# Where the expert biases are prepared, which expert groups come first, and how the smallest groups use the PE columns in a decoder layer

## The chip, the core and the metric

The kernel runs on one core of a Trainium2 chip. Its engines are TensorE (PE, with its weight loads shown apart as PEld), VectorE (DVE), ScalarE (ACT), GpSimd (POOL) and SyncE (SP), which here issues all DMA transfers. The metric is the device time of one execution in microseconds; smaller is better. The profile's rows show the TensorE clock as a granted share of 2.4 GHz: 1.00, or 0.50, which is 1.2 GHz.

## The reference

One decoder layer on 256 tokens of width 1024: a mixer (8 heads of forgetting attention and 4 mLSTM heads, then one output product), cross-attention into 256 memory tokens, and a top-4-of-32 mixture of experts, each followed by a layer norm of `alpha*x + part`. Cut to what matters here:

```python
mixed = jnp.concatenate([fo, mo_out], axis=-1)          # (256, 1024)
x = layer_norm(ALPHA * x + mixed @ w_out, ln1_g, ln1_b)
x = layer_norm(ALPHA * x + cross_attention(x, mem), ln2_g, ln2_b)
logits = x @ w_router + b_router                        # (256, 32)
top_vals, top_idx = lax.top_k(logits, 4)
gates = softmax(top_vals)
for e in range(32):                                     # the tokens that chose e
    h = xe @ w_gate_up[e] + b_gate_up[e]                # 1024 -> 2048
    g, l = minimum(h[:, :1024], 7), clip(h[:, 1024:], -7, 7)
    y[tokens] += gate * ((g * sigmoid(1.702 * g) * (l + 1)) @ w_down[e] + b_down[e])
x = layer_norm(ALPHA * x + y, ln3_g, ln3_b)
```

All weights are float32. One expert has 12 MiB of them: 8 MiB gate/up and 4 MiB down.

## The kernel before

**Slots and the weight stream.** SBUF holds 24 slots of 1 MiB (`NU = 24`). `big()` takes the slot that has been free longest, `done()` puts slots back at the end of that list. All large tiles live there: weight chunks, their split halves, activations, the table of expert biases `bgf`. Weights come as a stream of 1 MiB chunks in a fixed order (`stream`): the projections, the two *static* experts 0 and 1 (16 gate/up chunks, then 8 down chunks), and then the other experts in an order found at run time, each one's 8 gate/up chunks ahead of the previous one's 4 down chunks. `pump()` takes a slot for the next chunk and issues its DMA on SP's queue (L143 to L149) as long as slots are free. SP works in order: a DMA into a slot whose last user isn't done holds up everything that SP issues after it. Which instruction comes when on each engine is fixed ahead of time by a scheduler that goes by program order; `tc.high_priority(offset=-300)` makes instructions rank as if they stood 300 places later, a positive offset as if they stood earlier.

**Front.** Projections, the head groups, the mixer's output product with the first layer norm (from L640 on, `take_sq`, `apply_N`, `stats`, `layer_norm`), cross-attention (`queries`, `xattn`), its output product (`attn_out`) and the router (`logits`, `router`). Float32 products of the front are made of three products of split halves: `split()` makes the high half on ACT (L173) and the low half on DVE (L176).

**Expert biases.** `b_gate_up` is added by a bf16 matmul with a selector column (L1196), so the float32 table is cut into three bf16 parts on partitions 0 to 63, 64 to 95 and 96 to 127 of `bgu`. Before the change the table is loaded after the second half of the cross-attention (L744), and POOL cuts it into parts during the attention's output product (L820 to L823). The first expert's bias matmuls read `bgu`.

**Experts.** The tokens of an expert are put into a group of 32, 64, 96 or 128 places (T, S, M, B). After the routing, experts are ranked by their count of tokens, and the 32 groups of the table `BATCHES` are given to them by size; each batch has 256 places (the first 128), and the order in the table is the order of work. The 32nd group is worked on only if its expert has tokens, so 31 run. `gate_up(i)` makes bias and gate/up product with the tokens as the stationary operand and the weights as the moving one, 512 columns at a time: for 64 places two column halves of PE work side by side (`128*64`), for 32 places four quarters (`128*32`), for 128 places the whole array. M runs as S and T. `turned(i)` transposes the hidden rows into `hT` (a half slot, always at its start), and `product(i-1)` multiplies by the down weights; T has only two column groups there, on partitions 0 to 31 and 32 to 63. ACT and DVE copy the two output halves into `y`. `fillers(i)` between experts makes the one-hot matrices, gathers the next batch's tokens (L918), scatters finished rows into the result (L1113), and after item 2 starts the accumulator (`start_acc`).

Of the kernel before, what the change touches and what calls it, by code (L numbers as in the profile page):

```python
# [12 lines left out]
BF = mybir.dt.bfloat16  # L13
I32 = mybir.dt.int32
AF = mybir.ActivationFunctionType
ALU = mybir.AluOpType
# [5 lines left out]
KT = 8  # L22
# [8 lines left out]
NSTATIC = 2  # L31
T, S, M, B = 32, 64, 96, 128

BATCHES = [[S] * NSTATIC, [S, S, M, T], [B, T, T, T, T], [S, S, M, T], [B, S, S], [M, T, S, S], [M, T, S, S],
           [M, T, T, T, T, T]]
NU = 24
NT2 = 8
# [12 lines left out]
def layer_kernel(ctx, tc, x, mem, w_in, fox_f_bias, conv_w, i_bias, f_bias, fox_g, mlstm_g, w_mix,  # L50
                 ln1_g, ln1_b, w_xq, w_xk, w_xv, w_xo, ln2_g, ln2_b, w_router, b_router,
                 w_gu, b_gu, w_dn, b_dn, ln3_g, ln3_b, out):
    nc = tc.nc
# [6 lines left out]
    cp = ctx.enter_context(tc.tile_pool(name="cp", bufs=1))  # L60
# [14 lines left out]
    def big(shape, dt=F32, last=False):  # L75

        i = free.pop(-1 if last else 0)
        t = up.tile(shape, dt, name=nm("u"), tag=f"u{i}")
        owner[id(t)] = (i, t)
        return t  # L80

    def done(*ts):
        for t in ts:
            free.append(owner.pop(id(t))[0])
# [12 lines left out]
    def t2(shape, dt=F32):  # L97
        return wk.tile(shape, dt, name=nm("t2"), tag="t2", bufs=NT2)
# [484 lines left out]
    done(vmo, fvm)  # L583


    def stats(t, n, st):

        ve.bn_stats(st[:, n], xs[:, t, 512 * n:512 * n + 512])
        if n == 0:
            return  # L590
        mv = sm([128, 2])
        ve.bn_aggr(mv, st)
        rs = sm([128, 2])
        se.activation(rs[:, 0:1], mv[:, 1:2], AF.Ln, bias=eps_l)
        se.activation(rs[:, 1:2], rs[:, 0:1], AF.Exp, scale=-0.5)
        return mv[:, 0:1], rs[:, 1:2]
# [7 lines left out]
    def take_sq(W=None, n=4, ahead=4, reserve=2):  # L604

        W = W or ([], [])
        for i in range(n):
            ch = take()
            pump(taken[0] + ahead, reserve)
            with tc.high_priority(offset=-300):  # L610
                W[0].append(split(ch, 4, 512))
            W[1].extend(W[0][-1])
        return W
# [25 lines left out]

    ln1 = load_ln(ln1_g, ln1_b)  # L640
    W, Wh = take_sq()
    pump(taken[0] + 4)
    sts = [sm([128, 2, 6]) for _ in range(2)]
    for n in range(2):
# [94 lines left out]
    heads(1)  # L739
    Wo[0, 1] = take_xo()  # L740
    done(qT)
    bgf = big([128, 2048])
    for q in range(4):
        nc.sync.dma_start(bgf[32 * q:32 * q + 32], b_gu)  # L744
    pump(len(stream), 2)


# [67 lines left out]
    ve.tensor_scalar(rsum, pb[:, 0], -1.0, None, op0=ALU.mult)  # L815
    ve.tensor_copy(brow_, pb[:, 1])
    ve.tensor_tensor(wr, wr, g2[:, :, None].to_broadcast([128, KT, NE]), op=ALU.mult)

    bgu = cp.tile([128, 2048], BF, name="bgu", tag="shared")
    gp.tensor_copy(bgu, bgf)  # L820
    for q in (64, 96):
        gp.tensor_tensor(bgf[q:], bgf[q:], bgu[q:], op=ALU.subtract)
        gp.tensor_copy(bgu[q:], bgf[q:])  # L823
    done(bgf)

    gp.memset(lgx, -3e38)
    gdpos = cp.tile([128, 2, 2, NE], F32, name="gdpos")
    pump(len(stream))
# [324 lines left out]
        given[0] += 1  # L1153
        pump(1 << 20, held_back[0] if given[0] > 4 else 0)

    def transposed(hid):

        out_, at = [], 0
        hT = half_slot(0)
        for hh in hid:  # L1160
            n = hh.shape[0]
            p = bank((4, 5), [128, 4, n])
            for j in range(4):
                te.transpose(p[:, j], hh[:, j * 128:(j + 1) * 128], ident[0:n, 0:n])  # L1164
            o = hT[:, at:at + 4 * n].rearrange("p (k s) -> p k s", s=n)
            se.copy(o, p)  # L1166
            out_.append(o)
            at += 4 * n
        return out_
# [49 lines left out]
        hidden[i] = hid  # L1219

    def turned(i):
        hidden[i] = transposed(hidden[i])

    def product(i):

        b, o = starts[i]
        c = flat[i]
        gk = (b, o // 128)
        hT = hidden.pop(i)
        if gk not in Y:  # L1230
            Y[gk] = half_slot(1)
            if i == nitem - 1:
                gp.memset(Y[gk], 0.0)
            elif gk == (len(BATCHES) - 1, 1):
                gp.memset(Y[gk][96:128], 0.0)  # L1235
        y = Y[gk]
        work = []
        for m, (a, n) in enumerate(parts(c)):
            if n == B:
                p = [bank((4, 5), [128, 512]) for _ in range(2)]  # L1240
                work.append((a, n, p, lambda k: hT[k // 4][:, k % 4]))
            else:
                p = bank((4, 5), [128, 512])
                work.append((a, n, [p[n * h:n * h + n] for h in range(2)],
                             lambda k, m=m, n=n: hT[m][:, k % 4, n * (k // 4):n * (k // 4) + n]))
        for k2 in range(KT // 2):
            cd = next_chunk()
            for a, n, p, w in work if k2 % 2 == 0 else work[::-1]:
                for kk in range(2):
                    k = 2 * k2 + kk  # L1250
                    for h in range(2):
                        te.matmul(p[h], w(k), cd[:, kk, 512 * h:512 * h + 512], start=(k == 0), stop=(k == KT - 1),  # L1252
                                  skip_group_check=True)
            give(cd)
        for a, n, p, _ in work:
            q = (o + a) % 128
            se.copy(y[q:q + n, 0:512], p[0])  # L1257
            ve.tensor_copy(y[q:q + n, 512:1024], p[1])  # L1258
        if (o + c) % 128 == 0 or i >= nitem - 2:
            pend.append(gk)  # L1260
# [212 lines left out]
```

## Time and profile before

| what | value |
|---|---|
| median of 3 runs | 1217.68 us (1217.25 to 1220.58) |
| profiled execution | 1217.34 us, span of its instructions 1215.5 us |
| mean granted TensorE clock | 0.975 |
| PE / DVE / ACT / POOL busy share of the span | 94% / 31% / 19% / 4% |
| HBM read | 428.18 MB |

The span runs from the first to the last instruction of the program; 1.84 us of the profiled execution lie around it. All places in time below are microseconds from the span's start. In a row of the timeline, the last bracket is the engine's idle time before the instruction and what ended it. A matmul that is written once in the program appears as two instructions when its operands are float32. Several matmuls overlap in the array, so the time of a run of them is read from the row's total, not from one instruction.

### The profile page before, as it was taken

The page shows a single profiled execution, that of the slowest core. Times are in us where ns is not written, and L with a number is a line of the kernel's source. Part 1 is how long each engine was busy: PE and PEld are TensorE (multiplying, and loading weights), DVE is VectorE, ACT ScalarE, POOL GpSimd, SP SyncE. Part 2 cuts the span into 40 slices and gives each one's busy share as a digit, 9 for nine tenths or more (in the row PEclk, how much of TensorE's full clock was granted, in tenths as well). Part 3 has the DMA queues.
Part 4 walks back from the last instruction along what each step waited for, and adds up shares of the span by engine and source line. Part 5 has one row for each costly group of instructions (what it writes and reads, how often), then busy time and mean ns, then how long its engine had stood idle before and what let it go on. Part 6 is the DMA issues. An engine that isn't in the chain of part 4 may idle for free.

```text
span 1215.5 us, 14844 instructions
## 1 busy us (share of the span) xinstructions
PE 1141.2 (94%) x5825; PEld 524.4 (43%) x5826; DVE 376.9 (31%) x775; ACT 230.9 (19%) x429; POOL 49.2 (4%) x79
## 2 busy tenths in 40 slices
PE   9999999979999999999899899999999999999875
PEld 8997678855443334332223333433233323322211
DVE  6674656462323120421120302222211222122212
ACT  5545534311200110111001100110111010100101
POOL 3320000040000000000000000000000000000000
PEclk9999999987998999999999999999999999999888
DMA  8763328576999999999999999999999999999994
GB/s 284 273 224 123 139 99 304 224 243 218 375 377 372 416 401 360 377 417 417 417 417 416 417 417 417 417 417 416 417 417 417 416 417 417 416 417 417 417 416 176
DMA packets 92104, 430.25 MB, mean 354 GB/s; under 512 B 11152, under 2 KB 11704, under 8 KB 60158
## 3 DMA queue, kind: packets, MB, share of 16 engines
q1 hardware_dynamic: 92030, 429.26, 88.7%
q8 instruction: 47, 0.77, 0.3%
q14 instruction: 27, 0.22, 0.0%
HBM read 428.18 MB, written 1.05 MB: 353 GB/s over the span
## 4 chain that ended last, share of the span: by engine, by line
PE 76%; DMA 17%; DVE 5%; ACT 1%; issue 1%; SPq 0%; DVEq 0%; ACTq 0%
PE ps L1202 28%; PE ps L1252 18%; PE ps L195 14%; DMA u<-in_w_gate_up_dram 10%; DMA u<-in_w_down_dram 7%; PE ps L1113 4%; PE ps L918 2%; PE ps L1164 1%; DVE t L1132 1%; PE ps L1196 1%; PE ps L694 1%; PE ps L715 1%; PE ps L513 1%; DMA u<-in_w_mix_out_dram 1%; PE ps L478 1%
## 5 line engine op out<-in xcount | busy, mean ns | idle before, releaser
L1202 PE MATMUL ps<-u,u 128*64 128x512 f32 (+2 forms) x2304 | 441.6, 604 | 13.4 <-DMA u<-in_w_gate_up_dram 13.2
L1252 PE MATMUL ps<-u,u 128*64 128x512 f32 (+2 forms) x1152 | 287.3, 601 | 5.3 <-DMA u<-in_w_down_dram 2.4
L1202 PEld LDWEIGHTS ps<-u,u 128*64 128x64 f32 (+2 forms) x2304 | 136.0, 127 | 283.6 <-issue 223.7
L195 PE MATMUL ps<-u,u 128*128 128x256 f32 (+1 forms) x1152 | 200.8, 327 | 0.5 <-DVE u L184 0.5
L195 PEld LDWEIGHTS ps<-u,u 128*128 128x128 f32 x1152 | 165.7, 191 | 20.3 <-issue 3.3
L1252 PEld LDWEIGHTS ps<-u,u 128*64 128x64 f32 (+2 forms) x1152 | 79.7, 127 | 169.4 <-issue 147.8
L1128 DVE TENSOR_SCALAR t<-ps 128x512 f32<-128x512 f32 (+1 forms) x38 | 26.1, 686 | 377.2 <-PE ps L1202 377.2
L1258 DVE COPY u<-ps 64x512 f32<-64x512 f32 (+2 forms) x36 | 24.8, 690 | 262.6 <-ACT u L1257 238.1
L1130 ACT ACTIVATE t<-t 128x512 f32<-128x512 f32 (+1 forms) x38 | 23.9, 630 | 343.8 <-DVE t L1128 343.8
L176 DVE TENSOR_TENSOR u<-u,u 128x1024 fp32r<-128x1024 f32 x58 | 74.2, 1310 | 19.8 <-ACT u L173 13.7
L173 ACT CAST u<-u 128x1024 fp32r<-128x1024 f32 x64 | 64.9, 1049 | 40.7 <-PE ps L195 16.2
L1257 ACT COPY u<-ps 64x512 f32<-64x512 f32 (+2 forms) x36 | 20.7, 576 | 249.9 <-PE ps L1252 233.7
L1113 PE MATMUL ps<-u,gt 128*128 128x512 f32 x112 | 59.3, 639 | 5.4 <-ACT u L1257 5.4
L1115 DVE TENSOR_TENSOR u<-u,ps 128x512 f32<-128x512 f32 x56 | 38.5, 687 | 57.6 <-PE ps L1113 57.6
L923 ACT ACTIVATE u<-ps,pcol 128x256 f32<-128x256 f32 (+1 forms) x60 | 29.9, 553 | 73.3 <-PE ps L918 63.7
L918 PE MATMUL ps<-t,u 128*128 128x256 f32 (+1 forms) x256 | 41.3, 307 | 0.2 <-ACT u L923 0.2
L1196 PE MATMUL ps<-bgu,selb 128*64 128x512 bf16 (+2 forms) x143 | 25.8, 397 | 16.2 <-DVE t L1132 15.5
L918 PEld LDWEIGHTS ps<-t,u 128*128 128x128 f32 x256 | 34.4, 199 | 15.1 <-issue 10.4
L1166 ACT COPY u<-ps 128x512 f32<-128x512 f32 (+1 forms) x38 | 18.6, 488 | 93.4 <-PE ps L1164 93.1
L1113 PEld LDWEIGHTS ps<-u,gt 128*128 128x128 f32 x112 | 18.5, 193 | 39.7 <-issue 14.9
L1235 POOL MEMSET u<- 32x1024 f32 x1 | 0.9, 947 | 844.6 <-PE ps L1113 844.6
L1164 PEld LDWEIGHTS ps<-ident,t 128*128 128x128 f32 (+1 forms) x152 | 14.4, 139 | 31.9 <-issue 16.8
(274 smaller groups left out, 609.6 us busy)
## 6 DMA issues: line engine op xcount, KB each, us to landing
u<-in_w_gate_up_dram SPq DMA_DIRECT2D x248, 1024.0 KB
u<-in_w_down_dram SPq DMA_DIRECT2D x122, 1024.0 KB
u<-in_w_in_dram SPq DMA_DIRECT2D x20, 512.0 KB
u<-in_w_xk_dram SPq DMA_DIRECT2D x4, 1024.0 KB
u<-in_w_xv_dram SPq DMA_DIRECT2D x4, 1024.0 KB
u<-in_w_mix_out_dram SPq DMA_DIRECT2D x4, 1024.0 KB
u<-in_w_xq_dram SPq DMA_DIRECT2D x4, 1024.0 KB
u<-in_w_xo_dram SPq DMA_DIRECT2D x4, 1024.0 KB
```

Source lines behind the costliest of these rows:

```text
L173: a = se.copy(h[:, sl], c[:, sl])
L176: b = eng.tensor_tensor(l[:, sl], c[:, sl], h[:, sl].bitcast(F32), op=ALU.subtract)
L195: m = te.matmul(out, wsl(wp[a]), xsl(xp[b]), start=(first and i == 0), stop=(last and i == 2), skip_group_check=True)
L918: te.matmul(p[:, j], s[:, t, k * 128:(k + 1) * 128], oh[b][:, t], start=(t == j == i == 0), stop=(t == 1 and s is src[-1]), skip_group_che ...
L923: a = se.activation(xg[b][:, k, 0:cols], p[:, j], AF.Identity, scale=g2[:, k:k + 1], bias=b2[:, k:k + 1])
L1113: te.matmul(p, gth[gk][:, t], y[:, 512 * n:512 * n + 512], start=True, stop=True)
L1115: ve.tensor_add(a, a, p)
L1128: ve.tensor_scalar(g, G, LIMIT, None, op0=ALU.min)
L1164: te.transpose(p[:, j], hh[:, j * 128:(j + 1) * 128], ident[0:n, 0:n])
L1196: te.matmul(out_[q], selb[:, r:r + 1].to_broadcast([128, n]), bgu[:, 512 * q:512 * q + 512], start=True, stop=False, skip_group_check=True)
L1202: te.matmul(out_[q], X[:, k, o + a:o + a + n], ch[:, 512 * q:512 * q + 512], start=False, stop=(k == KT - 1), skip_group_check=True)
L1252: te.matmul(p[h], w(k), cd[:, kk, 512 * h:512 * h + 512], start=(k == 0), stop=(k == KT - 1), skip_group_check=True)
```

## The change

Three edits, made together. The table `b_gate_up` is loaded ahead of the first layer norm's rows, and ScalarE and VectorE cut it into its parts, in four column quarters, in the low rank that the splits also have; POOL's code for it is gone. The table of batches is in another order, so that four T and two S follow the static pair, and the two B stand later (positions 12 and 19 in place of 6 and 15); the sizes are the same. The down product of a T group uses four column groups: even `k` on partitions 0 to 63, odd `k` on 64 to 127; ACT copies the second sum to SBUF and DVE adds the two, half by half. Hidden rows of items of up to 64 places go to the two halves of `hT`'s half slot by turns.

```diff
-BATCHES = [[S] * NSTATIC, [S, S, M, T], [B, T, T, T, T], [S, S, M, T], [B, S, S], [M, T, S, S], [M, T, S, S],
+BATCHES = [[S] * NSTATIC, [T, T, T, T, S, S], [M, T, S, S], [B, M, T], [S, S, M, T], [B, S, S], [M, T, S, S],
            [M, T, T, T, T, T]]
...
+    bgu = cp.tile([128, 2048], BF, name="bgu", tag="shared")
+    bgf = big([128, 2048])
+    for q in range(4):
+        nc.sync.dma_start(bgf[32 * q:32 * q + 32], b_gu)
+
+    def bias_parts():
+        for n in range(4):
+            h = slice(512 * n, 512 * n + 512)
+            se.copy(bgu[:, h], bgf[:, h])
+            for q in (64, 96):
+                ve.tensor_tensor(bgf[q:, h], bgf[q:, h], bgu[q:, h], op=ALU.subtract)
+                se.copy(bgu[q:, h], bgf[q:, h])
+        done(bgf)
...
     ln1 = load_ln(ln1_g, ln1_b)
     W, Wh = take_sq()
+    with tc.high_priority(offset=-300):
+        bias_parts()
     pump(taken[0] + 4)
...
-    bgf = big([128, 2048])
-    for q in range(4):
-        nc.sync.dma_start(bgf[32 * q:32 * q + 32], b_gu)
     pump(len(stream), 2)
...
-    bgu = cp.tile([128, 2048], BF, name="bgu", tag="shared")
-    gp.tensor_copy(bgu, bgf)
-    for q in (64, 96):
-        gp.tensor_tensor(bgf[q:], bgf[q:], bgu[q:], op=ALU.subtract)
-        gp.tensor_copy(bgu[q:], bgf[q:])
-    done(bgf)
...
-        hidden[i] = transposed(hidden[i])
+        hidden[i] = transposed(hidden[i], 512 * (i % 2) if flat[i] <= S else 0)
...
-                work.append((a, n, [p[n * h:n * h + n] for h in range(2)],
+                work.append((a, n, [p[n * h:n * h + n] for h in range(128 // n)] + [p[64:128]],
...
-                        te.matmul(p[h], w(k), cd[:, kk, 512 * h:512 * h + 512], start=(k == 0), stop=(k == KT - 1),
+                        te.matmul(p[h + (2 * kk if n == T else 0)], w(k), cd[:, kk, 512 * h:512 * h + 512],
+                                  start=(k2 == 0 if n == T else k == 0), stop=(k2 == 3 if n == T else k == KT - 1),
                                   skip_group_check=True)
...
+            if n == T:
+                r = t2([128, 512])[0:64]
+                se.copy(r, p[4])
+                for h in range(2):
+                    ve.tensor_add(y[q:q + n, 512 * h:512 * h + 512], p[h], r[32 * h:32 * h + 32])
+                continue
```

## Rows read from the trace of the kernel before

**Rows 1.** The page: the span, the busy time of each engine (share of the span, instructions), and in 40 equal slices of the span the busy share of the DMA engines in tenths and what they moved.

```profile
span 1215.5 us, 14844 instructions
PE 1141.2 (94%) x5825; PEld 524.4 (43%) x5826; DVE 376.9 (31%) x775; ACT 230.9 (19%) x429; POOL 49.2 (4%) x79
DMA  8763328576999999999999999999999999999994
GB/s 284 273 224 123 139 99 304 224 243 218 375 377 372 416 401 360 377 417 417 417 417 416 417 417 417 417 417 416 417 417 417 416 417 417 416 417 417 417 416 176
```

**Rows 2.** Windows in the experts' stage: from:to, length, then busy time (and instructions) of PE, PEld, DVE, ACT and POOL, the granted TensorE clock, the DMA engines' busy share, and GB/s.

```profile
299.00:346.00 47.00, 47.00 (x230) 22.07 (x228) 12.23 (x30) 10.54 (x21) 0.00 (x0) 1.00 0.93 356
346.00:358.00 12.00, 12.00 (x56) 6.19 (x53) 0.72 (x2) 0.17 (x1) 0.00 (x0) 1.00 1.02 415
358.00:378.00 20.00, 20.00 (x50) 5.86 (x52) 9.65 (x15) 0.46 (x1) 0.00 (x0) 0.83 0.89 360
470.00:500.00 30.00, 30.00 (x105) 11.19 (x103) 6.44 (x10) 2.79 (x5) 0.00 (x0) 1.00 0.89 323
346.00:520.00 174.00, 170.70 (x763) 62.02 (x761) 44.33 (x93) 18.00 (x34) 0.00 (x0) 0.98 0.98 389
520.00:1190.00 670.00, 629.15 (x3088) 203.53 (x3088) 135.71 (x251) 71.60 (x134) 0.95 (x1) 0.98 1.02 417
```

**Rows 3.** Waits of SP's queue between 315 and 510: whom it waited for, us in total, times, longest.

```profile
SPq L149 <- PE ps L1202: 100.7, 47, 9.0
SPq L149 <- PE ps L1252: 50.6, 23, 5.9
```

**Rows 4.** PE's timeline in the experts' stage: start, length, line, operation, out<-in, stationary and moving shapes, count.

```profile
315.53 7.09 PE L1202 MATMUL ps<-u,u 128*64 128x512 f32 x32
...
337.11 7.41 PE L1252 MATMUL ps<-u,u 128*64 128x512 f32 x32
...
369.36 5.23 PE L1113 MATMUL ps<-u,gt 128*128 128x512 f32 x8
...
440.41 4.50 PE L1202 MATMUL ps<-u,u 128*32 128x512 f32 x40
...
461.19 14.00 PE L1202 MATMUL ps<-u,u 128*128 128x512 f32 x32
...
489.45 4.49 PE L1252 MATMUL ps<-u,u 128*32 128x512 f32 x20
```

**Rows 5.** POOL's timeline around the cutting of the bias table.

```profile
234.37 0.20 POOL L764 MEMSET rt<- 128x128 bf16 x1 [162.79 <-ACT t L701]
...
258.56 4.06 POOL L822 TENSOR_TENSOR u<-u,bgu 32x2048 f32<-32x2048 f32 x1
262.68 1.97 POOL L823 CAST bgu<-u 32x2048 bf16<-32x2048 f32 x1
```

**Rows 6.** DVE's timeline in the router.

```profile
245.53 0.42 DVE L760 TENSOR_SCALAR t<-t 1x512 f32<-1x512 f32 x1
...
258.24 0.69 DVE L622 SCALAR_TENSOR_TENSOR u<-u,ps 128x512 f32<-128x512 f32 x1 [0.92 <-PE ps L195]
258.96 3.94 DVE L760 TENSOR_SCALAR t<-t 1x512 f32<-1x512 f32 x1
262.93 2.00 DVE L862 TENSOR_SCALAR u<-u,sm,sm 128x512 f32<-128x512 f32 x1
264.86 0.17 DVE L810 COPY sm<-ps 2x32 f32<-2x32 f32 x1
...
274.35 0.55 DVE L862 TENSOR_SCALAR u<-u,sm,sm 128x512 f32<-128x512 f32 x1 [1.07 <-PE ps L840]
```

**Rows 7.** PE's timeline in the router.

```profile
250.25 0.66 PE L840 MATMUL ps<-ident,u 128*128 128x128 f32 x4
...
265.08 1.06 PE L812 MATMUL ps<-sm,ident 2*128 2x32 f32 x4 [5.88 <-DVE sm L810]
...
273.20 1.11 PE L840 MATMUL ps<-ident,u 128*128 128x128 f32 x4 [0.28 <-DVE gdpos L884]
...
284.82 2.07 PE L918 MATMUL ps<-t,u 128*128 128x128 f32 x8
...
291.13 1.16 PE L918 MATMUL ps<-t,u 128*128 128x128 f32 x8
```

**Rows 8.** Windows in the front, columns as in rows 2: heads and mixer output, and the stretch from the router's first PE work after an idle time to the first expert's product.

```profile
152.00:182.00 30.00, 28.45 (x130) 21.09 (x130) 17.70 (x52) 11.63 (x25) 0.00 (x0) 1.00 0.27 96
265.08:286.80 21.72, 18.08 (x82) 15.12 (x82) 7.92 (x48) 3.29 (x8) 0.61 (x2) 0.50 0.74 290
```

**Rows 9.** ACT's timeline in the front: a copy of 128x512 elements out of PSUM, and the first splits of the layer norm's stretch.

```profile
142.75 0.59 ACT L460 COPY u<-ps 128x512 f32<-128x512 f32 x1 [1.93 <-PE ps L195]
...
180.14 2.00 ACT L173 CAST u<-u 128x1024 fp32r<-128x1024 f32 x2 [6.20 <-PE ps L195]
```

**Rows 10.** All engines' timeline at the end of the run.

```profile
1171.09 1.94 PE L1202 MATMUL ps<-u,u 128*32 128x512 f32 x8 [1.40 <-DMA u<-in_w_gate_up_dram]
...
1181.11 0.68 DVE L1133 TENSOR_TENSOR t<-t,t 64x512 f32<-64x512 f32 x1
...
1200.07 0.57 ACT L1257 COPY u<-ps 32x512 f32<-32x512 f32 x1 [7.64 <-PE ps L1252]
1200.67 0.69 DVE L1258 COPY u<-ps 32x512 f32<-32x512 f32 x1 [7.92 <-ACT u L1257]
```

More of the change, by code (lines that the diff above doesn't have):

```diff
@@ L1154, in give, with transposed @@
         pump(1 << 20, held_back[0] if given[0] > 4 else 0)
-    def transposed(hid):
-        out_, at = [], 0
+    def transposed(hid, at=0):
+        out_ = []
         hT = half_slot(0)
```

## The prediction

> **What bounds the kernel now.** I read the page first. PE is 94% busy [rows 1], which looks like the bound, but the line of transfer rates says more: from the 18th of the 40 slices on, the stream moves 416 to 417 GB/s in every slice to the last but one, and its engines are full. In that part, 520 to 1190 us, the DMA share is 1.02 [rows 2], so the experts are bound by their weights there; PE is busy because it waits inside its stream of chunks. A chunk of 1 MiB takes 1.0486 MB / 417 GB/s = 2.51 us, an expert of 12 chunks 30.2 us. The bytes are the same after the change. So the end moves by two things alone: how much earlier the stream becomes full, and how much of the time after that it loses before 520 us.
>
> The windows then give the losses, as length x (1 - rate/417). From 299 to 346 us: 47 x (1 - 356/417) = 6.9 us. From 346 to 520: 174 x (1 - 389/417) = 11.7 us, of it 2.7 us in 358 to 378 and 6.7 us in 470 to 500 [rows 2]. What holds the stream in that time is told by SP's waits: 100.7 us for gate/up matmuls and 50.6 us for down matmuls [rows 3]. SP has no free slot until PE gives a chunk back. So up to some 510 us PE is the bound, and after it the stream.
>
> PE's own prices come from its timeline [rows 4]. S gate/up: 32 instructions in 7.09 us, 64 make 14.2; S product 7.4; T gate/up 40 in 4.50, 64 make 7.2; T product 20 in 4.49, 32 make 7.2; B gate/up 28.0. An S expert is 21.6 us, a T 14.4, an M (S and T) 36.0, a B some 42; a batch's gather and two scatters (5.23 each) add about 16. The old second and third batch, S S M T and B T T T T, need 110 and 116 us of PE, the M and the B within them 36 and 42 each against the stream's 30.2: the B is the loss of 470 to 500.
>
> Before 299 us a chain bounds the kernel: router, first gather, first gate/up product, which gives back the first slots. In the router there is a hole. PE idles 5.88 us and waits for a copy on DVE [rows 7]. DVE had done its work at 258.9, and then came a scaling of one row in 3.94 us and a normalisation in 2.00 us; the same lines take 0.42 and 0.55 us elsewhere [rows 6]. Both slow ones end within 0.3 us of the end of a POOL instruction that cuts the bias table (258.56 + 4.06 = 262.62, 262.68 + 1.97 = 264.65) [rows 5].
>
> **The change part by part.**
>
> *POOL's cutting goes.* DVE gets back 3.94 - 0.42 = 3.5 us and 2.00 - 0.55 = 1.45 us, together 5.0 us of the idle 5.88 [rows 6, 7]. I take 5.0; the bounds are 0 (another operand of the router is late next, the scaled router weights that follow on DVE) and 5.9. The hole is followed by a stretch at clock 0.50, the 1.2 GHz level, from PE's return to the first experts' product [rows 8]. Four transposes there take 1.11 us against 0.66 just before, and eight gathers 2.07 against 1.16 just after [rows 7]: a factor of 0.58. PE is busy 18.1 us of that stretch, so the full clock throughout would save 18.1 x 0.42 = 7.6 us, and a clock that falls all the same saves nothing. With the hole at 1 us I expect the fall to come later or to last shorter and take the middle, 3.8 us. Together 8.8 us, all of it on the chain and so passed on to the stream's start. The slot of the bias table is also held for less of this stretch, but at its end the same 24 slots are full, so that gives nothing.
>
> *The cutting on ACT and DVE.* Twelve copies at 0.59 us [rows 9] make 7.1 us of ACT, eight subtractions at 0.68 [rows 10] 5.4 us of DVE. The last reader of the buffer that `bgu` shares is the last head's matmul, so they fall from about 152 us on. From 152 to 182 ACT is busy 11.6 of 30 us and DVE 17.7 [rows 8], and ACT is idle for 6.2 us in a piece ahead of 180 [rows 9]. They rank low, so most go into those holes while PE works on the output product. What is queued behind one is the layer norm's own small steps, for which x's transposes and then PE wait. I take 1.0 us of delay. Bounds: 0, and 5.4 us if all subtractions fall into the layer norm's chain. The table's load moves to before the first layer norm's rows; all later tiles take the next slot, the second query chunk one that comes free after the heads instead of during them. It is split some 20 us after that, and the DMA queue moves only 96 GB/s from 152 to 182 [rows 8]: nothing.
>
> The Trainium skill, "SBUF — State Buffer", section "Who interferes with whom", says that DVE and POOL lock a shared port pair for a whole instruction, and DVE's two-operand subtractions contend with POOL too. By it the subtractions would stretch in their new place if POOL read there. POOL's row shows 162.8 us of idle time up to 234 [rows 5], so by it too they cost 0.68 us each.
>
> *T first.* Batch 0 is unchanged, S S, so the 6.9 us of 299 to 346 stay; bounds 0 and a gain of 4 us, if `hT`'s two halves let transposes go ahead of a product (PE shows no idle time here to win [rows 2], so I take 0). Then the old item 2 gave back 8 slots in 14 us, and PE was held from 358 to 374.6 by the accumulator's start and the first scatter [rows 2, 4]. A T gives the 8 back in 7.2 us, 5 more than the stream uses in that time; with two given back during the hold that covers its 16.6 us (6.6 chunks). After it, T needs 10.8 us of PE for 30.2 us of stream. The lead batch is 4 x 10.8 + 2 x 21.6 + 16 = 102 us of PE for 72 chunks or 181 us of stream. PE catches up within it and waits from there. The two B come later: S S, then B M, is 43.2 + 42 + 32.4 + 16 = 134 us for 120.7 of stream, a lag of 13 us from a start at 0. Of the 24 slots 18 hold chunks by then, 45 us of stream, so the lag costs nothing; the old second B, at a time when PE was level with the stream, cost nothing either (last of [rows 2]). I take the whole 11.7 us; bounds 4 and 11.7.
>
> *Four column groups.* T's product falls from 7.2 to 3.6 us, as T's gate/up shows that four groups run at 0.112 us an instruction [rows 4]. For 12 T and 5 M that is 61 us of PE, but in every place PE waits for the stream then; it covers the cost and takes the gain, so I count 0. In its place comes evacuation: ACT copy, then two additions. At the end of the run that is on the path: today copy 0.57 and copy 0.69 follow each other [rows 10], then 0.57 + 2 x 0.69: +0.7 us. The last chunk's own matmuls run two groups wide as before.
>
> The Trainium skill, "TensorEngine Tiling (Array Packing)", "PSUM Bottleneck", speaks against this edit: tiling speeds up TensorE but not evacuation, which may become the bound. By it a T would cost 1.95 us of evacuation against 1.26, on engines that are busy 19 and 31% of the span [rows 1]; the sum would carry only the same 0.7 us at the end.
>
> **Sum.** The profiled execution is 1217.34 us, 0.34 under the median. 1217.3 - 5.0 - 3.8 + 1.0 - 11.7 + 0.7 = 1198.5, beside the median 1198.9: I say 1199 us. A change of 0.3% is 3.7 us, about what a measurement of this kernel can tell from none.
>
> **The rivals.**
>
> A. *The catch-up is only half.* PE carries its lag into S S B M and the stream stalls at the moved B as it did at 470. For it: the first B cost 6.7 us [rows 2]. Against it: six cheap experts go ahead. It returns 6.7 us and the onehots of six items instead of four delay the gather by some 1 us: 1207.
>
> B. *The layer norm pays.* The cutting sits in the chain, 5.4 us instead of 1.0, and the clock falls in the router anyway (3.8 us): 1199 + 4.4 + 3.8 = 1207.
>
> C. *The hole and the stall are not on the path.* Other operands are late in the router, and the stream loses its 11.7 us in other places: about 1216, no change.
>
> D. *Slower: the clock in the lead batch.* PE, waiting for chunks, falls to 1.2 GHz and stays there through S S M. At the end of the run it does so for a time: eight T matmuls take 1.94 us [rows 10] instead of 4.50 x 8/40 = 0.90 [rows 4]. A T at half clock still fits into 30 us, but S at 43 us and M at 65 would lag 13 + 13 + 35 = 61 us. From 45 us, the slots' worth, it costs: 16 us; with B and M following at that clock another 54 + 35, some 100 in all, against which the gain of 18 us is small. It decides only if the clock stays low during dense work; 520 to 1190 has 0.98 with the same waits in it [rows 2]. With S S M alone low, 1199 + 16 = 1215; with the B as well some 1270.
>
> **How the numbers follow.** Forecast 0.64, with its own range 1192 to 1204 (clock 0 or 7.6, delay 0 to 5.4). A 0.13, B 0.12, C 0.06, D 0.05, of which 0.04 is slower. The low end, 1190, is 1199 - 3.8 - 1.0 - 4; the high end, 1210, takes in A and B with some of each other. Beyond it lie C, D and tails of A and B. Faster by over 0.3%: 0.64 + 0.13 + 0.12 = 0.89, plus 0.01 of D; within 0.3%: 0.06; slower 0.04.
>
> **What would show it.** Right: no long DVE row and no 5 us hole in the router; the first expert's product some 8 us earlier; 417 GB/s from about 340 us on; SP waiting for DMAs, not for PE, from the lead batch on; T products at 0.112 us an instruction. Wrong: a window under 400 GB/s after 360 us (A); layer-norm steps on DVE later by more than 2 us against the heads (B); PE's clock at 0.50 through S and M after the lead batch (D).

## The result, and the profile after

| | before | after |
|---|---|---|
| median of 4 runs | 1217.47 us (1214.88 to 1220.58) | 1190.22 us (1188.12 to 1190.68) |
| ratio | | 0.9772 [0.9746, 0.9798] |
| profiled execution, its span | 1217.34, 1215.5 us | 1188.12, 1186.3 us |

The change takes 27.3 us off the median where 18.7 were forecast. 1190.2 is at the low edge of the range, 1190 to 1210, and outside the forecast's own 1192 to 1204.

The page of after: span, busy times, DMA share and GB/s in 40 slices; it answers [rows 1].

```profile
span 1186.3 us, 14910 instructions
PE 1093.6 (92%) x5826; PEld 492.9 (42%) x5826; DVE 388.8 (33%) x800; ACT 238.3 (20%) x441; POOL 35.6 (3%) x74
DMA  8757148678899999999999999999999999999994
GB/s 288 283 188 238 37 143 302 261 304 305 328 416 417 417 417 415 417 417 417 417 417 417 417 417 417 417 417 418 416 417 417 417 416 418 417 415 418 416 416 161
```

The stream is full from the 12th slice on instead of the 18th. The windows say the same more closely. SP issues the 25th expert chunk, the one that waits for the first slot the first expert product gives back, at 280.5 us instead of 299.2, so [rows 2] are answered by windows that start 18.7 us earlier. The fourth and fifth are the heads with the mixer's output, and the router (columns as in rows 2):

```profile
280.50:327.50 47.00, 46.82 (x236) 19.32 (x234) 12.81 (x37) 10.23 (x20) 0.00 (x0) 1.00 0.92 356
327.50:501.50 174.00, 153.34 (x844) 46.53 (x836) 44.64 (x78) 17.09 (x33) 0.00 (x0) 0.93 1.02 417
501.50:1160.00 658.50, 611.97 (x3011) 200.30 (x3010) 145.78 (x275) 73.93 (x137) 0.95 (x1) 0.97 1.02 417
152.00:182.00 30.00, 26.68 (x118) 20.48 (x119) 21.99 (x49) 17.76 (x32) 0.00 (x0) 1.00 0.55 193
248.75:268.20 19.45, 18.59 (x121) 14.86 (x121) 12.24 (x53) 4.70 (x12) 1.40 (x4) 1.00 0.83 331
```

The first batch still loses 47 x (1 - 356/417) = 6.9 us, the next 174 us lose nothing where they lost 11.7. In these 174 us SP waits 89.8 us for transfers and 31.9 us for PE; in the window of before, 346 to 520 us, all of its 132.9 us of waiting were for PE. The router runs at a granted clock of 1.00 (2.4 GHz), where [rows 8] had 0.50 for nearly the same busy time of PE, 18.1 us.

PE's timeline in the router of after (L847 transposes, L853 logits, L925 gather, L1209 first expert product; L195 is the attention's output product). Compare [rows 7]:

```profile
246.75 0.63 PE L823 MATMUL ps<-t,pcol 128*2 128x32 f32 x16
...
250.15 1.17 PE L195 MATMUL ps<-u,u 128*128 128x512 f32 x4
251.16 0.99 PE L853 MATMUL ps<-t,t 128*128 128x32 f32 x8
251.98 1.84 PE L195 MATMUL ps<-u,u 128*128 128x512 f32 x7
...
259.84 0.60 PE L847 MATMUL ps<-ident,u 128*128 128x128 f32 x4
...
266.90 1.16 PE L925 MATMUL ps<-t,u 128*128 128x128 f32 x8
...
268.23 1.02 PE L1209 MATMUL ps<-u,u 128*64 128x512 f32 x2
```

The idle 5.88 us are gone. But something else is new: row sums (L823) and the logits of the first 128 tokens stand *among* the output product's matmuls, not behind the last of them. The order of PE's instructions is another, and the first expert product starts at 268.2 instead of 287.1 us.

### The profile page after: what moved, and what is told of

It is laid out like the page before. It is cut to its first block, busy times and chain, and to the rows that moved or that the text cites. A ratio compares the mean times of both kernels' runs of the same rounds, so it can differ in the third digit from the quotient of the medians.

```text
span 1186.3 us, 14910 instructions
## 1 busy us (share of the span) xinstructions
PE 1093.6 (92%) x5826; PEld 492.9 (42%) x5826; DVE 388.8 (33%) x800; ACT 238.3 (20%) x441; POOL 35.6 (3%) x74
## 4 chain that ended last, share of the span: by engine, by line
PE 63%; DMA 15%; DVE 5%; ACT 1%; issue 0%; SPq 0%; DVEq 0%; ACTq 0%
PE ps L1209 31%; PE ps L1260 15%; DMA u<-in_w_gate_up_dram 8%; DMA u<-in_w_down_dram 6%; PE ps L1120 5%; PE ps L195 4%; PE ps L925 3%; DVE t L1139 1%; PE ps L1171 1%; PE ps L1203 1%; PE ps L712 1%; PE ps L733 1%; PE ps L1352 1%; DVE t L1140 1%; DVE t L1141 1%; PE ps L1108 1%
## 5 line engine op out<-in xcount | busy, mean ns | idle before, releaser
L1209 PE MATMUL ps<-u,u 128*32 128x512 f32 (+2 forms) x2304 | 446.0, 615 | 24.7 <-DMA u<-in_w_gate_up_dram 24.7
L1209 PEld LDWEIGHTS ps<-u,u 128*32 128x32 f32 (+2 forms) x2304 | 128.6, 128 | 310.2 <-issue 237.2
L1260 PE MATMUL ps<-u,u 128*32 128x512 f32 (+2 forms) x1152 | 239.0, 621 | 14.1 <-DMA u<-in_w_down_dram 11.6
L195 PE MATMUL ps<-u,u 128*128 128x256 f32 (+1 forms) x1152 | 203.0, 327 | 4.6 <-ACT u L509 1.8
L195 PEld LDWEIGHTS ps<-u,u 128*128 128x128 f32 x1152 | 164.5, 190 | 24.6 <-issue 3.2
L1135 DVE TENSOR_SCALAR t<-ps 128x512 f32<-128x512 f32 (+1 forms) x38 | 26.1, 686 | 381.5 <-PE ps L1209 381.5
L1260 PEld LDWEIGHTS ps<-u,u 128*32 128x32 f32 (+2 forms) x1152 | 63.5, 128 | 146.1 <-issue 106.2
L176 DVE TENSOR_TENSOR u<-u,u 128x1024 fp32r<-128x1024 f32 x58 | 74.5, 1311 | 16.2 <-ACT u L173 13.4
L1270 DVE TENSOR_TENSOR u<-ps,t 32x512 f32<-32x512 f32 x34 | 23.2, 683 | 118.8 <-ACT t L1268 118.4
L1273 DVE COPY u<-ps 64x512 f32<-64x512 f32 (+1 forms) x19 | 13.2, 693 | 108.9 <-ACT u L1272 87.1
L925 PEld LDWEIGHTS ps<-t,u 128*128 128x128 f32 x256 | 32.5, 190 | 14.9 <-issue 11.4
L925 PE MATMUL ps<-t,u 128*128 128x256 f32 (+1 forms) x256 | 38.2, 293 | 0.0
L1139 DVE TENSOR_SCALAR t<-ps 128x512 f32<-128x512 f32 (+1 forms) x38 | 26.3, 692 | 3.7 <-PE ps L1209 3.2
```

What stands on the lines that cost most here:

```text
L176: b = eng.tensor_tensor(l[:, sl], c[:, sl], h[:, sl].bitcast(F32), op=ALU.subtract)
L195: m = te.matmul(out, wsl(wp[a]), xsl(xp[b]), start=(first and i == 0), stop=(last and i == 2), skip_group_check=True)
L925: te.matmul(p[:, j], s[:, t, k * 128:(k + 1) * 128], oh[b][:, t], start=(t == j == i == 0), stop=(t == 1 and s is src[-1]), skip_group_che ...
L1139: ve.tensor_scalar(l, L, LIMIT, -LIMIT, op0=ALU.min, op1=ALU.max)
L1209: te.matmul(out_[q], X[:, k, o + a:o + a + n], ch[:, 512 * q:512 * q + 512], start=False, stop=(k == KT - 1), skip_group_check=True)
L1260: te.matmul(p[h + (2 * kk if n == T else 0)], w(k), cd[:, kk, 512 * h:512 * h + 512], start=(k2 == 0 if n == T else k == 0), stop=(k2 == 3 ...
```

## The experiments

The labels are those of the runs. "Stretch" is the time from SP's issue of the 13th expert chunk to the first matmul of the first expert product, in the profile; "loss" is what the stream loses in the 174 us that begin 47 us after its 25th chunk. The ratio is to runs of before taken beside the kernel, whose medians stayed between 1217.1 and 1217.7 us. The 13th chunk is the last of this row of SP's timeline, and starts 0.4 us before the row ends, at 230.5 us in before (first line) and at 228.1 in after:

```profile
189.03 41.91 SPq L149 DMA_DIRECT2D u<-in_w_gate_up_dram  x13
...
185.41 43.11 SPq L149 DMA_DIRECT2D u<-in_w_gate_up_dram  x13
```

The first product starts at 287.06 us in before and at 268.23 in after.

| kernel | what is in it | median (range), us | ratio to before | stretch | loss |
|---|---|---|---|---|---|
| before | nothing of the change | 1217.5 (1214.9 to 1220.6) | | 56.5 | 11.6 |
| after | all | 1190.2 (1188.1 to 1190.7) | 0.9772 [0.9746, 0.9798] | 40.1 | 0.2 |
| old_bias | order, groups | 1206.7 (1203.9 to 1207.7) | 0.9901 [0.9870, 0.9933] | 56.0 | 0.3 |
| cut_late | all, but loaded and cut late | 1204.9 (1202.3 to 1206.3) | 0.9894 [0.9866, 0.9922] | 55.7 | 0.2 |
| pool_cuts | all, but POOL cuts | 1196.3 (1195.7 to 1197.8) | 0.9823 [0.9795, 0.9851] | 40.1 | 0.1 |
| dummy4 | all, and a dead late load | 1197.3 (1196.6 to 1198.0) | 0.9846 [0.9822, 0.9871] | 48.0 | 0.2 |
| wr_first | old_bias, router weights first | 1200.8 (1198.3 to 1204.7) | 0.9874 [0.9839, 0.9909] | 50.7 | 0.1 |
| hole_warm | dummy4 with 16 idle matmuls | 1195.4 (1193.6 to 1198.3) | 0.9814 [0.9787, 0.9841] | 46.4 | 0.1 |
| old_order | bias, groups | 1196.0 (1191.3 to 1198.0) | 0.9812 [0.9774, 0.9850] | 41.3 | 3.6 |
| two_groups | bias, order | 1193.0 (1191.3 to 1193.9) | 0.9804 [0.9778, 0.9830] | 41.4 | 0.4 |
| bias_only | bias | 1200.1 (1198.6 to 1200.5) | 0.9864 [0.9839, 0.9889] | 41.7 | 12.5 |
| one_half | all, `hT` always at its start | 1189.1 (1188.0 to 1190.1) | 0.9766 [0.9739, 0.9793] | 40.1 | 0.2 |
| product_first | all, and one call moved | 1188.6 (1187.5 to 1188.8) | 0.9760 [0.9738, 0.9783] | 41.5 | -0.1 |

### What shortens the router

**old_bias**: the table is loaded and cut by POOL as before; order and groups stay new.

```diff
-    with tc.high_priority(offset=-300):
-        bias_parts()
...
     done(qT)
+    bgf = big([128, 2048])
+    for q in range(4):
+        nc.sync.dma_start(bgf[32 * q:32 * q + 32], b_gu)
...
+    gp.tensor_copy(bgu, bgf)
+    for q in (64, 96):
+        gp.tensor_tensor(bgf[q:], bgf[q:], bgu[q:], op=ALU.subtract)
+        gp.tensor_copy(bgu[q:], bgf[q:])
```

> The changed kernel with the bias table as before: loaded after the second half of the cross-attention, cut by POOL during the attention's output product. New order of experts and new T product stay. In the changed kernel the first gate/up matmul stands at 268.2 us, before at 287.1. If the bias edit is the whole cause of that, it returns to 287 and the time is 1190 + 18.8 = 1209 us. Rival: the other two edits also move the front (other one-hots, other orders on the engines); then the first gate/up matmul stands well before 287 and the time is under 1206.

Measured 1206.7 us; the stretch is back at 56.0, the clock at 0.50 for 24 us from 261 on. The bias edit is worth 16.5 us on top of the other two. The first product is at 285.7 us, not quite the 287 of the first theory; 1206.7 lies between the two theories' times.

**pool_cuts**: the table is loaded early, but POOL cuts it, by the code of before in its old place.

```diff
-    with tc.high_priority(offset=-300):
-        bias_parts()
...
+    gp.tensor_copy(bgu, bgf)
...
```

> The changed kernel with the load of the bias table early, as changed, but cut by POOL at the old place in the program. Theory order: the early load takes the table out of SP's queue ahead of the router's weights, and with them early the router's products stand among those of the attention's output in PE's fixed order; then most of the gain of the front stays, first gate/up at 268 to 273 us, time 1190 to 1195, clock 1.00 in the router. Theory contention: the gain of the front is POOL's hold on DVE and the low clock after the hole that it makes; with POOL cutting again the hole and the clock of 0.50 return, first gate/up at 280 or later, time 1202 or more.

Measured 1196.3 us, stretch 40.1, clock 1.00 in the router: what the theory of the order expects there, though the time is 1.3 us over its range. With the table there, POOL cuts in the heads, at 145 to 163 us. Its timeline, DVE's beside it, and a window of that time:

```profile
147.02 4.93 POOL L823 TENSOR_TENSOR u<-u,bgu 64x2048 f32<-64x2048 f32 x1
154.94 5.02 POOL L823 TENSOR_TENSOR u<-u,bgu 32x2048 f32<-32x2048 f32 x1
```

```profile
147.94 4.04 DVE L542 TENSOR_SCALAR sm<-sm 128x2 f32<-128x2 f32 x1
156.88 4.16 DVE L176 TENSOR_TENSOR u<-u,u 128x1024 fp32r<-128x1024 f32 x1
...
163.06 1.21 DVE L176 TENSOR_TENSOR u<-u,u 128x1024 fp32r<-128x1024 f32 x1
```

```profile
152.00:167.00 15.00, 8.81 (x21) 6.14 (x22) 14.87 (x23) 5.38 (x10) 10.63 (x3) 0.54 0.20 70
```

L542 ends with POOL's subtraction, to 0.03 us (147.94 + 4.04 beside 147.02 + 4.93), L176 takes 4.16 us beside the second one and 1.21 behind it; PE is busy 8.8 of 15 us and at 0.54. The 13th chunk comes at 235.8 instead of 228.1: POOL's hold, with a fall of the clock of 14 us, costs 7.7 us here (6.1 by medians). The router keeps its 40.1 us with no work of ACT or DVE on the table at all, so who cuts is not what makes it short.

**cut_late**: ACT and DVE cut with the code of after, but the load and the cutting stand where the kernel before has them.

```diff
-    with tc.high_priority(offset=-300):
-        bias_parts()
...
     done(qT)
+    bgf = big([128, 2048])
...
+    with tc.high_priority(offset=-300):
+        for n in range(4):
+            h = slice(512 * n, 512 * n + 512)
+            se.copy(bgu[:, h], bgf[:, h])
...
     gp.memset(lgx, -3e38)
```

> The changed kernel with the table loaded late, as before, and cut by ACT and DVE (not POOL) at the old place in low rank. Theory order: PE's order of before, with the router after the attention's output product, returns; without POOL's hold the hole is under 2 us, so some 5 us of the 18.8 stay and the clock's share if it doesn't fall (up to 7.6): first gate/up at 275 to 282 us, time 1197 to 1204. Theory contention: nearly the whole gain stays, first gate/up at 268 to 271, time 1190 to 1193.

Measured 1204.9 us, stretch 55.7, first product at 282.2 us: neither theory's time. POOL holds nobody, and the stretch is as long as old_bias's. PE's timeline in the router:

```profile
258.81 1.06 PE L813 MATMUL ps<-sm,ident 2*128 2x32 f32 x4 [3.68 <-DVE sm L811]
...
266.62 0.59 PE L1199 MATMUL ps<-bgu,selb 128*64 128x512 bf16 x1 [2.21 <-ACT bgu L826]
268.71 0.19 PE L884 MATMUL ps<-rt 128*128 128x32 bf16 x1 [1.51 <-DVE sm L870]
```

The cutting itself now stands among the router's steps on DVE, and PE's order is the old one, with all logits behind the output product.

So the early *load* matters, apart from the cutting. SP's timeline before, where the table's load L744 stands ahead of the router's weights (L799), and SP's wait in that time:

```profile
231.84 0.23 SPq L759 DMA_DIRECT2D t<-in_ln_g_dram  x1
243.17 2.04 SPq L744 DMA_DIRECT2D u<-in_b_gate_up_dram  x4
...
246.39 0.40 SPq L799 DMA_DIRECT2D t<-in_w_router_dram  x1
```

```profile
SPq L744 <- DVE u L176: 11.1, 1, 11.1
```

And of after:

```profile
236.24 0.40 SPq L814 DMA_DIRECT2D t<-in_w_router_dram  x1
```

SP stood 11.1 us for a slot, the router's weights behind it. With the load gone from there they are issued 10 us earlier, and the fixed order has the row sums and the first logits among the output product. Two kernels test from both sides whether the place of the load does that.

**dummy4**: after, and at the old place a second load of the table that nothing reads. DVE and POOL have nothing to cut in the router.

```diff
     done(qT)
+    bgd = big([128, 2048])
+    for q in range(4):
+        nc.sync.dma_start(bgd[32 * q:32 * q + 32], b_gu)
...
+    done(bgd)
     gp.memset(lgx, -3e38)
```

> The changed kernel, table cut early by ACT and DVE, and at the old place of the table's load a second load of it into a slot that nothing reads; POOL and DVE have nothing to cut in the router. SP again stands for a slot ahead of the router's weights, and PE's fixed order has the router's logits behind the attention's output product, as before. Theory 'SP's order decides the router': from the stream's 13th chunk to the first expert product about 50 to 56 us (40.1 in the changed kernel, 56.6 before), the clock at 0.50 for some 15 to 25 us, time 1200 to 1206 us. Theory 'POOL's cutting held DVE and that alone made the stretch long': 40 to 43 us as in the changed kernel, 1190 to 1193 us. The prediction's own price (POOL's hold 5.0 and half of the clock's 7.6 in the old order) would be 56.6 - 8.8 = 48 us, 1198 us.

Measured 1197.3 us, stretch 48.0. SP's timeline, PE's, and a window over the fall of the clock:

```profile
240.77 2.13 SPq L762 DMA_DIRECT2D u<-in_b_gate_up_dram  x4
...
244.08 0.40 SPq L817 DMA_DIRECT2D t<-in_w_router_dram  x1
```

```profile
255.63 0.60 PE L851 MATMUL ps<-ident,u 128*128 128x128 f32 x4
256.15 0.63 PE L826 MATMUL ps<-t,pcol 128*2 128x32 f32 x16
257.69 0.63 PE L830 MATMUL ps<-sm,ident 2*128 2x32 f32 x4 [0.91 <-DVE sm L828]
...
258.80 1.97 PE L857 MATMUL ps<-t,t 128*128 128x32 f32 x16
...
276.13 1.02 PE L1213 MATMUL ps<-u,u 128*64 128x512 f32 x2
```

```profile
261.00:275.00 14.00, 10.99 (x52) 8.61 (x50) 6.29 (x40) 3.02 (x7) 0.58 (x2) 0.52 0.72 286
```

PE's order in the router is the old one: row sums and all logits of the first tokens behind the output product. The hole is 0.91 us instead of 5.88; the clock falls for 14 us instead of 24. This kernel is what the prediction had in mind, and it gives 56.5 - 48.0 = 8.5 us, against the 8.8 of the sum. Against old_bias, which has the same order of batches and the same groups, it gives 56.0 - 48.0 = 8.0. Neither theory was right alone: some 8 us are POOL's hold with its share of the clock, and 48.0 - 40.1 = 7.9 us more are the order. The dead load also takes a slot and 1 MiB of DMA; PE shows no wait for a transfer in the stretch.

**wr_first**: the opposite, old_bias with only the router's weights moved.

```diff
     heads(1)
+    wr = t2([128, KT, NE])
+    nc.sync.dma_start(wr, w_router.rearrange("(k p) e -> p k e", p=128))
     Wo[0, 1] = take_xo()
...
-    wr = t2([128, KT, NE])
-    nc.sync.dma_start(wr, w_router.rearrange("(k p) e -> p k e", p=128))
```

> The new order of batches and four groups, the bias table loaded and cut by POOL at the old place (1206.7 us, 56.0 us from the 13th chunk to the first expert product), with one edit: the load of the router's weights is issued ahead of the table's. POOL's cutting still falls on the router. PE's fixed order then has the row sums and one half of the logits ahead of the last matmul of the attention's output. Theory 'SP's order decides the router': a part of the 16 us comes back, 48 to 53 us, 1199 to 1204 us. Theory 'POOL's cutting': DVE's long instructions and PE's idle time stay, 55 to 57 us, 1205 to 1208 us.

Measured 1200.8 us, stretch 50.7 against 56.0: 5.3 us from the place of one load, with POOL's cutting where it was; it lies in the range of the theory of SP's order. The clock's fall is 14 us here instead of 24, and its share of the 5.3 us is not told apart. The row sums now stand among the output product, at 244.8 us, the logits of the first 128 tokens only before its last few matmuls, and PE still idles behind them:

```profile
261.06 0.99 PE L846 MATMUL ps<-t,t 128*128 128x32 f32 x8
...
268.85 0.18 PE L881 MATMUL ps<-rt 128*128 128x32 bf16 x1 [6.16 <-DVE rt L878]
```

**hole_warm**: dummy4 with matmuls that nobody reads, to see what of the 7.9 us is the clock.

```diff
                 last = logits(t, n)
+                for _ in range((4, 12)[n] if t == 0 else 0):
+                    after(te.matmul(warm2, onesb, rt[:, 0:128].bitcast(BF), start=True, stop=True), last)
```

> The kernel with the second, dead load of the table (dummy4: 48.0 us from the 13th chunk to the first expert product, clock at 0.50 for 14 us of it, 1197.25 us) with 16 matmuls more whose result nothing reads, bf16 128x256, behind the logits of the first 128 tokens, so that PE does not idle there. PE's order is otherwise that of the kernel before. Theory 'what is left of the serial router's price is mostly the clock': the clock stays at 1.00, the stretch shrinks by about 12 us of busy PE time x 0.42 = 5 us to 43 to 44 us, 1192 to 1194 us. Theory 'it is the chain itself, DVE and ACT steps that no matmul covers': 47 to 50 us, 1196 to 1199 us, also if the clock stays up.

Measured 1195.4 us, stretch 46.4, between the two theories; the ranges of the two kernels overlap. The clock still fell, for 7 us instead of 14, and the added matmuls took 3.8 us of PE, so this settles nothing. From dummy4's window the clock can be worth at most 10.99 x 0.42 = 4.6 us (an estimate, with the factor 0.58 of the prediction); how the 7.9 us divide into clock and chain stays open.

### What keeps the stream full

**old_order**: after with the old table of batches.

```diff
-BATCHES = [[S] * NSTATIC, [T, T, T, T, S, S], [M, T, S, S], [B, M, T], ...
+BATCHES = [[S] * NSTATIC, [S, S, M, T], [B, T, T, T, T], [S, S, M, T], ...
```

> The changed kernel with the old table of batches (S S M T, then B T T T T after the static pair). The prediction's step: up to some 500 us PE is the bound again and the stream loses its 11 us; time 1201 us, first gate/up still at 268. Rival: with the front 19 us earlier the stream's loss comes from somewhere else, and the order is worth under 4 us: time under 1194.

**two_groups**: after with a T's down product in two column groups.

```diff
-                work.append((a, n, [p[n * h:n * h + n] for h in range(128 // n)] + [p[64:128]],
+                work.append((a, n, [p[n * h:n * h + n] for h in range(2)],
...
-            if n == T:
-                r = t2([128, 512])[0:64]
-                se.copy(r, p[4])
...
```

> The changed kernel with the down product of a T group in two column groups again and its old evacuation; the early table and the new order of batches stay. Theory 'the order alone carries the stream' (the prediction's count of 0 for the four groups): the stream still loses under 1 us in the 174 us behind its first 47, the time is that of the changed kernel, 1190 us (1188 to 1193). Rival 'the groups carry a part': PE's T costs 10.8 us instead of 7.2 in its product and gate/up half beside the gather and the scatter, the loss comes back by 3 us or more, 1193 to 1198.

**bias_only**: both of these edits together.

> The changed kernel with the old order of batches and two column groups: of the change only the early cutting of the bias table (and the two halves of hT) is left. Beside it stands the kernel with the old order and four groups, 1196.0 us, whose stream lost 3.6 us where the kernel before lost 11.6. Theory 'groups and order stand in for one another': without both the loss is back at some 11 us, time 1196 + 8 = 1204 us (1201 to 1206). Rival 'the earlier start of the stream did it, not the groups': the loss stays at 3 to 5 us, 1195 to 1198.

Measured: old_order 1196.0 us (loss 3.6), two_groups 1193.0 (0.4), bias_only 1200.1 (12.5). Without new order and groups the loss is what it was before, so the earlier start does not cure it. Four groups in the old order cut it to 3.6, the new order with two groups to 0.4. Against the expectations: old_order is at neither 1201 nor under 1194; two_groups keeps the small loss of its first theory, at the edge of that theory's time; bias_only has the loss of its first theory and is 0.9 us faster than its range. But two_groups loses later what after keeps. Its windows, then SP's waits from 880 to 1100 us in it:

```profile
840.00:880.00 40.00, 39.55 (x150) 16.09 (x149) 11.45 (x20) 3.64 (x6) 0.00 (x0) 1.00 1.02 415
880.00:920.00 40.00, 39.54 (x161) 16.31 (x160) 8.84 (x24) 6.56 (x13) 0.00 (x0) 1.00 1.01 402
920.00:960.00 40.00, 38.95 (x213) 12.16 (x211) 7.73 (x12) 3.96 (x7) 0.00 (x0) 1.00 1.01 405
...
1080.00:1100.00 20.00, 20.00 (x123) 5.39 (x124) 3.40 (x6) 0.63 (x2) 0.00 (x0) 1.00 0.93 376
```

```profile
SPq L149 <- PE ps L1209: 89.5, 51, 5.7
SPq L149 <- PE ps L1260: 62.4, 29, 5.2
```

In the same stretch of after most of the waiting is for transfers:

```profile
SPq L149 <- DMA u<-in_w_down_dram: 60.9, 31, 2.7
SPq L149 <- DMA u<-in_w_gate_up_dram: 59.6, 39, 2.0
SPq L149 <- PE ps L1260: 12.4, 7, 3.4
```

With two groups the stream waits for PE again from 880 us on; that profile loses 6.8 us there. By medians the steps are: bias edit 1217.2 to 1200.1 (-17.1), new order to 1193.0 (-7.2), four groups to 1190.2 (-2.7). In the old order the groups give -4.2. In both orders the intervals of the ratios with and without groups overlap, so the 2.7 us are shown by the place of the loss more than by their size.

**one_half**: after with `hidden[i] = transposed(hidden[i])` as before.

> The changed kernel with the hidden rows of every item at the start of the half slot again, as before, so that the two halves no longer take turns. The prediction counted them at 0 (bounds 0 and 4 us). Theory 'nothing': 1190 us (1188 to 1192), the stream's loss in the first 47 us stays 6.9. Rival 'transposes wait for the product': the loss there or in the next 174 us grows by 1 us or more, 1191.5 to 1194.

Measured 1189.1 us, loss in the first 47 us 7.2: the two halves of `hT` are worth nothing, as counted.

**product_first**: item 0's product ahead of the one-hot matrices and gathers of item 1.

```diff
+        if i == 1:
+            product(0)
         fillers(i)
...
-        if i and i != NSTATIC:
+        if i > 1 and i != NSTATIC:
             product(i - 1)
```

> The changed kernel with the down product of item 0 moved ahead of the one-hot matrices and gathers that stand between items 1 and 2, so that its four chunks are given back sooner. Theory 'the 6.9 us that the stream loses in its first 47 us are PE work that gives no slot back': the loss falls to 3 to 5 us, time 1186.5 to 1188.5 us. Rival 'the gather of the next batch becomes late instead' (its tokens wait for the same one-hot matrices): the first T starts as much later as the product starts earlier, 1190 to 1193 us.

Measured 1188.6 us (1187.5 to 1188.8). The loss in the first 47 us falls from 6.9 to 4.0, and from the 25th chunk to the last the profile is 2.8 us shorter; its front was 2.7 us longer, with the clock down for 3 us in the heads and 3 in the router. Against after's 1190.2 the gain is 1.7 us by medians, with ratios that overlap: that the loss falls is seen in one profile, the gain in time is likely and not shown.

## Why the prediction was right or wrong

By profiles, in us:

| term | forecast | measured |
|---|---|---|
| up to the 13th chunk (cutting on ACT and DVE) | +1.0 | -2.4 |
| router: POOL's hold, and its clock | -8.8 | -8.5 (before to dummy4) |
| router: SP's and PE's order | none | -7.9 (dummy4 to after) |
| the stream's first 47 us | 0 | 0 (6.9 both times) |
| the next 174 us | -11.7 | -11.4 |
| from the last chunk to the end | +0.7 | +0.3 |

The measured terms make -29.9; the spans part by 29.2, with small terms between, and the medians by 27.3; the profile of after is its fastest run. By medians the bias edit gave 17.1 us (bias_only) where the sum had 8.8 - 1.0 = 7.8, and order and groups gave 9.9 where it had 11.7 - 0.7 = 11.0. So the miss is in the bias edit.

**The step that failed** is "The table's load moves to before the first layer norm's rows; ... nothing." It followed the slot that the load takes, not the queue that it leaves. SP stood 11.1 us at L744 with the router's weights behind it, and the place of that load decides where the router's products stand in PE's fixed order (after and dummy4). That was a missing term of 7.9 us, most of the miss; how much of it is the clock stays open. The wait was in the trace of before, in SP's rows of the front, which the prediction did not use.

That 1190.2 lies in the range all the same is luck. Its low end was made of a full clock (3.8), a free cutting (1.0) and a gain of `hT`'s halves (4); the halves gave nothing (one_half), and 7.9 us came from a term that the sum did not have.

**POOL's hold** was right in kind and size: a hole of 0.91 us, so 5.0 less, and a shorter fall of the clock in dummy4, together 8.5 us beside 5.0 + 3.8. cut_late adds that it is the place of the cutting that costs: on ACT and DVE it is as dear there as on POOL.

**The cutting on ACT and DVE** was to cost 1.0 us. The 13th chunk came 2.4 us earlier, but that is no gain of the cutting. The kernels before, old_bias and cut_late have one order of matmuls up to some 250 us and issue that chunk at 230.5, 229.7 and 226.5 us. old_bias falls behind cut_late by 3.2 us between 148 and 159 us, where its clock is down twice for 3 us. The kernel before falls behind by 4.0 us between 95 and 101: a transfer lands later, ACT and then PE wait for it, and the clock falls for 3.5 us. Its ACT row; in cut_late the same row starts at 92.69 us, after 4.90 us of waiting:

```profile
95.33 1.99 ACT L173 CAST u<-u 128x1024 fp32r<-128x1024 f32 x2 [7.38 <-DMA u<-in_w_mix_out_dram]
```

The profiles with no fall of the clock up to that chunk are to be compared: 228.1 to 228.4 us with the early cutting on ACT and DVE (after, dummy4, one_half, bias_only, two_groups), 226.5 without it (cut_late). That is a cost of some 1.6 us, near the 1.0, with a single profile on one side. Rival B falls: its 5.4 us are not there, and after has no fall of the clock in the router.

The Trainium skill, "SBUF — State Buffer", section "Who interferes with whom", has DVE's two-operand instructions contend with a POOL instruction that reads SBUF. pool_cuts agrees, with L176's 4.16 us beside POOL's subtraction. By that rule it was right that cutting on DVE, with POOL idle, does not stretch: the eight subtractions of after take 0.685 to 0.690 us each.

**T first** was right in the sum, 11.4 of 11.7 us and 417 GB/s from 327.5 us on, and wrong in what it was put down to. The order alone (two_groups) recovers the loss of the 174 us and gives 6.8 back after 880 us.

**Four column groups** at 0 is a second step that did not hold, by 2.7 to 4.2 us of median: "in every place PE waits for the stream then" holds only because the groups make PE fast enough. The sum was not hurt by it, because "T first" was worked out with 10.8 us of PE for a T, and that is 7.2 + 3.6, the product in four groups already. A T's product runs at 2.78 us for 24 instructions, 0.116 each (first line). The evacuation at the end, by ACT and DVE, answers [rows 10]:

```profile
376.68 2.78 PE L1260 MATMUL ps<-u,u 128*32 128x512 f32 x24
...
1170.51 0.58 ACT L1268 COPY t<-ps 64x512 f32<-64x512 f32 x1 [9.46 <-PE ps L1260]
1171.12 1.40 DVE L1270 TENSOR_TENSOR u<-ps,t 32x512 f32<-32x512 f32 x2 [8.67 <-ACT t L1268]
```

0.58 + 1.40 = 1.98 us beside the 0.57 + 2 x 0.69 = 1.95 of the forecast. From the last chunk to the end after is 0.3 us longer; two_groups and bias_only, which end alike, part by 1.0, so this term can't be told from 0.

**The other rivals.** A asked for a window under 400 GB/s after 360 us: none. C fell with the first expert product at 268 us. D's fall of the clock happens, 0.93 as a mean of 327.5 to 501.5 us, but PE then waits for the stream and only 0.2 us are lost.

## What to carry to other kernels

When a DMA is moved on an in-order queue, read what stood *behind* it and how long it waited: here 8 us lay in the place of a small load behind a large one that had no slot. Where a scheduler fixes each engine's order, moving such a load can also change the order on other engines, and no duration in the trace of the old kernel gives the price of that; compare the order of both kernels first. And an edit that "only" speeds up an engine off the bound is worth what its slack buys later: undo it alone before calling it nothing.

## What the hardware showed that was not expected

While POOL subtracts 64x2048 elements (4.93 us), a DVE instruction on 128x2 elements took 4.04 us: it was held to POOL's end. Kernels with the same order of matmuls stood 3 to 4 us apart in the front, by a transfer that landed 2.6 us later and by falls of the clock of some 3 us each that come in one profile and not in another. Each kernel has one profile, so a term of the front under some 3 us is read only between profiles without such falls. And filling PE's idle time with matmuls came with a fall of 7 us instead of 14 in that stretch, but did not prevent it.
